# A gelu's inner product and a layer norm's factor and bias, from GpSimd to fused steps on VectorE

## The chip, the core and the metric

The kernel runs on one core of a Trainium2 chip. The metric is the time of one execution on the device in microseconds; a kernel's time is the median of several runs. The core's engines work side by side, each through its own list of instructions in order: TensorE (PE in the profile: matrix products, which need their weights loaded, PEld), VectorE (DVE), ScalarE (ACT), GpSimd (POOL) and SyncE (SP). They wait for each other through semaphores. TensorE writes to banks of PSUM; all else lies in SBUF. Transfers between memory and SBUF (DMA) are issued here from SyncE's and GpSimd's lists.

## What is computed

Two layers over 256 tokens of 2048 features. The first mixes a recurrence and a sparse attention; the second, which the change touches, is a gated unit. Its part of the reference:

```python
def odd_mixer(hn, w_in, ln_g, ln_b, w_s, b_s, w_out):
    u, v, g = jnp.split(hn @ w_in, 3, axis=-1)
    u = jax.nn.gelu(u)
    v = layer_norm(jax.nn.gelu(v), ln_g, ln_b)
    vc = v.reshape(bsz, n_chunks, SG_CHUNK, SG_GROUPS, SG_GROUP)
    mixed = jnp.einsum('gts,bcsgd->bctgd', ws, vc) + b_s.T[:, :, None]
    y = u * mixed.reshape(bsz, t, SG_WIDTH) * jax.nn.silu(g)
    return y @ w_out
```

The gelu is the tanh form, x (1 + tanh(c (x + a x^3))) / 2 with a = 0.044715. The layer norm takes the mean and the variance of each token over 2048 features, then a factor and a bias per feature. After each layer the input is joined by a gated embedding (`gate_layer`), with one more product by a 2048 x 2048 matrix.

## The kernel before, in words

**The weight stream.** Nearly all time goes to products of 256 tokens with wide weight matrices in float32, done in three fast passes: each operand is split in a high part (`hi`, `xh`) and a rest (`lo`, `xl`), and lines 169 to 171 add hi x xh, lo x xh and hi x xl. The weights come as a stream: SyncE loads 128 x 2048 numbers at a time (`raw`, line 128, five buffers), and each half of these is one chunk. For a chunk, ScalarE writes `hi` (line 137) and VectorE writes `lo = raw - hi` (line 138), each 128 x 1024 into one of four buffers; then TensorE has twelve matmuls on it (two token tiles, two weight tiles, three passes). Eight chunks make one unit, 512 features for all tokens, in two banks; its result goes to a background task.

**Background tasks.** Tasks are generators that `advance` moves one step for each chunk, so their instructions stand between those of the stream, on the same engines and in the same lists. The place in each engine's list is set by the order in which the program records them and by the scheduler of the tile framework.

**The second layer.** Four units give v (`ov_task`), four give u (`ou_task`), four the gate (`og_task`). Both `ov_task` and `ou_task` copy a unit's two tiles of 128 x 512 from the banks with the token's factor (`evac`, line 386) and call `gelu2` (line 696): ScalarE squares (702), VectorE scales and adds 1 (703), GpSimd multiplies by x (704), ScalarE takes the tanh (708), VectorE finishes (709). `ov_task` also gathers statistics on VectorE (720). When the fourth v unit is through, `ln` (726) turns these into a mean and a factor for each token, with a power on GpSimd (734); then for each of four column blocks `lng` and `lnb`, the factor and the bias for all partitions, are loaded from GpSimd's list (744), VectorE subtracts the mean and multiplies by the token's factor (748), and GpSimd multiplies by `lng` (749) and adds `lnb` (750). The first of these blocks fall into the time of the first u unit. `mix_task` needs both results; its first matmul (779) starts at 972.3 us of the profile.

Of the kernel before, what the change touches and what calls it, by code (L numbers as in the profile page):

```python
# [40 lines left out]
GELU_C = 0.7978845608028654  # L41
GELU_A = 0.044715

# columns of the packed parameter block
C_NG = 0
C_PG = 32
C_CW = 64
# [11 lines left out]
class Trunk:  # L59
# [13 lines left out]
        self.n = 0  # L73
        self.done = set()

# [1 line left out]
    def name(self, s):  # L77
        self.n += 1
        return f"{s}{self.n}"
# [13 lines left out]
    def pg(self, name="pg"):  # L93
        return self.psg.tile([128, 512], F32, tag="g", name=self.name(name))

# [1 line left out]
    def spawn(self, gen, delay=0):  # L97
        self.bg.append([delay, gen])

# [12 lines left out]
        while not all(k in self.done for k in keys):  # L112
            yield

# [1 line left out]
    def load(self, ap, cols):  # L116
        self.loads.append((ap, cols))
        return len(self.loads) - 1
# [29 lines left out]
            self.issue_split(self.next_split)  # L148
            self.next_split += 1

# [1 line left out]
    def unit(self, loads, acts, post, n=512, per_load=2, nk=KT, bank=None):  # L152
        st = {}
        bank = bank or self.pg
# [24 lines left out]
    def wunit(self, acts, post):  # L179
        self.unit([self.wl() for _ in range(4)], acts, post)  # L180

# [1 line left out]
    def split(self, src, gain=None, scale=None):  # L183
        """src [128 features, 2 tiles, 256 tokens] in two parts that the fast products carry exactly"""
        nc = self.nc
        hi = self.t(src.shape, F32R, "xh")
        lo = self.t(src.shape, F32R, "xl")
        if gain is not None:
            for s in range(2):
                g = gain[:, s:s + 1]  # L190
                nc.scalar.activation(hi[:, s], src[:, s], AF.Copy, scale=g)  # L191
                nc.vector.scalar_tensor_tensor(lo[:, s], src[:, s], g, hi[:, s].bitcast(F32),  # L192
                                               op0=OP.mult, op1=OP.subtract)
        elif scale is not None:
            nc.scalar.activation(hi, src, AF.Copy, scale=scale)
            nc.vector.scalar_tensor_tensor(lo, src, scale, hi.bitcast(F32), op0=OP.mult, op1=OP.subtract)
        else:
            nc.scalar.activation(hi, src, AF.Copy)
            nc.vector.tensor_tensor(lo, src, hi.bitcast(F32), op=OP.subtract)
        return hi, lo  # L200

    def fm(self, a0, a1, name="fm"):
        """token-major [128 tokens, 256] for both token tiles to [128 features, 2 tiles, 256 tokens] in a bank"""
        pt = self.pa(name)
        with self.tc.issue_after(self.last_mm.ins):
            for k in range(2):
                for t, x in ((0, a0), (1, a1)):
                    self.nc.tensor.transpose(pt[:, k * T + t * 128:k * T + (t + 1) * 128],  # L208
                                             x[:, k * 128:(k + 1) * 128], self.ident)
        return pt.rearrange("p (a b) -> p a b", a=2)  # L210

    def rms(self, ss, key):
        """ss [128 tokens, tile, part] of sums of squares"""
        nc = self.nc
        m = self.sm([128, 2])
        nc.vector.tensor_reduce(m, ss, axis=AX.X, op=OP.add)
        nc.vector.tensor_scalar(m, m, 1.0 / D, EPS, op0=OP.mult, op1=OP.add)  # L217
        r = self.kept([128, 4], "r" + key)
        nc.gpsimd.tensor_tensor(r[:, 0:2], m, self.mhalf[:, 0:2], op=OP.pow)  # L219
        nc.gpsimd.tensor_scalar(r[:, 2:4], r[:, 0:2], 0.5, None, op0=OP.mult)  # L220
        self.r[key] = r
        self.done.add("r" + key)
# [4 lines left out]
    def rth(self, key, t):  # L227
        return self.r[key][:, 2 + t:3 + t]

# [1 line left out]
    def consts(self):  # L231
        nc, a = self.nc, self.a
        self.cols = self.kept([128, C_ALL], "cols")
# [9 lines left out]
    def bias_table(self):  # L243
        nc, a = self.nc, self.a
        rel = self.kept([32, H], "rel")
        nc.gpsimd.dma_start(rel, a["rel_bias"])
        oh = self.kept([32, N_BUCKET_COLS], "oh")
        nc.gpsimd.dma_start(oh, a["onehot"])
        yield 4
        ps = self.pa("bt")  # L250
        with self.tc.issue_after(self.last_mm.ins):
            nc.tensor.matmul(ps[:H, :N_BUCKET_COLS], rel, oh, start=True, stop=True)
        sb = self.t([H, N_BUCKET_COLS], name="bt")
        nc.scalar.activation(sb, ps[:H, :N_BUCKET_COLS], AF.Copy)
        # row q of head h starts q elements further right: element (q, 127 + k) is the bias of key k
        bd = self.bias_d = self.dram.tile([H, 128, 512], F32, name="bias_d")
        yield
        nc.scalar.dma_start(bass.AP(tensor=bd.tensor, offset=bd.offset, ap=[[128 * 512, H], [513, 128], [1, 383]]),
                            sb[:, None, :383].to_broadcast([H, 128, 383]))
        self.done.add("bias")  # L260
# [26 lines left out]
        nc.vector.tensor_scalar(self.sp2, acc, 2.0, None, op0=OP.mult)  # L287
        nc.vector.tensor_scalar(self.spm4, acc, -4.0, None, op0=OP.mult)

# [1 line left out]
    def idx_task(self, i, ps):  # L291
        """the queries' own factor comes with iw, since relu(r x) = r relu(x) for r > 0"""
        nc = self.nc
        cp = lambda o, x: nc.scalar.activation(o, x, AF.Copy)
        if i == 0:
# [31 lines left out]
        yield  # L327

    def iq_task(self, j):
        """four heads"""  # L330
        nc = self.nc
        yield from self.until(f"iq{j // 2}")
        o = (j % 2) * T
# [44 lines left out]
        nc.vector.tensor_scalar(self.mb, sc, TAKEN_ABOVE, NEG, op0=OP.is_gt, op1=OP.mult)  # L378
        self.done.add("mask")

# [1 line left out]
    def evac(self, ps, key, name):  # L382
        out = []
        for t in range(2):
# [44 lines left out]
        self.done.add("v")  # L429
        yield  # L430

# [1 line left out]
    def q_task(self, g, ps):  # L433
        nc = self.nc
        qs = self.evac(ps, "x", "q")
# [87 lines left out]
        yield  # L523

    def gb_task(self, g, ps):
        """2 * silu without the token's factor, which comes with the attention"""
        nc = self.nc
        out = []
        for t in range(2):
            th = self.t(name="gb")  # L530
            nc.scalar.activation(th, ps[t], AF.Tanh, scale=self.rth("x", t))
            nc.vector.scalar_tensor_tensor(th, th, 1.0, ps[t], op0=OP.add, op1=OP.mult)
            out.append(th)
        self.sgb[g] = out
        self.done.add(f"gb{g}")
        yield

# [1 line left out]
    def ga_task(self, c, ps):  # L539
        nc = self.nc  # L540
        xs = self.evac(ps, "x", "ga")
# [82 lines left out]
        nc.vector.tensor_scalar(d, d, 0.0, -0.25, op0=OP.min, op1=OP.mult)  # L624
        st[p] = (a0, d, ti)

# [1 line left out]
    def squares(self, h, key, c, t):  # L628
        if c == 0 and t == 0:
            self.ss[key] = self.kept([128, 2, 4], "ss")  # L630
# [1 line left out]
        self.nc.scalar.activation(j, h, AF.Square, accum_out=self.ss[key][:, t, c:c + 1])  # L632

    def to_acts(self, hs, c, key, gain_col):
        """next products' operand; a step each"""
        for p in range(2):
            j = 2 * c + p
            o = p * T
# [53 lines left out]
        yield 2  # L692
        self.pT[layer] = {0: self.split(p)}

# [1 line left out]
    def gelu2(self, xs):  # L696
        """2 * gelu(x), in place, in steps"""
        nc = self.nc
        ys = []
        for x in xs:  # L700
            y = self.t(name="ge")
            nc.scalar.activation(y, x, AF.Square)  # L702
            nc.vector.tensor_scalar(y, y, GELU_A, 1.0, op0=OP.mult, op1=OP.add)  # L703
            nc.gpsimd.tensor_tensor(y, y, x, op=OP.mult)  # L704
            ys.append(y)
            yield
        for x, y in zip(xs, ys):
            nc.scalar.activation(y, y, AF.Tanh, scale=GELU_C)  # L708
            nc.vector.scalar_tensor_tensor(x, y, 1.0, x, op0=OP.add, op1=OP.mult)
            yield  # L710

# [14 lines left out]
    def ln(self):  # L726
# [12 lines left out]
        for c in range(4):  # L739
# [5 lines left out]
            yield  # L745
            for t in range(2):
                v = self.ov[c, t]
                nc.vector.tensor_scalar(v, v, mv[t][:, 0:1], sc[t][:, 1:2], op0=OP.subtract, op1=OP.mult)  # L748
                nc.gpsimd.tensor_tensor(v, v, g, op=OP.mult)
                nc.gpsimd.tensor_tensor(v, v, b, op=OP.add)  # L750
                yield
            self.done.add(f"vn{c}")

# [46 lines left out]
            self.y[2 * c + p] = self.split(self.fm(ys[0][:, o:o + T], ys[1][:, o:o + T], "yt"), scale=0.25)  # L800
        yield

# [1 line left out]
    def post(self, task, *args, delay=0):  # L804
        return lambda ps: self.spawn(task(*args, ps), delay)

# [188 lines left out]
```

## Time and profile before

| | |
|---|---|
| median of 3 runs | 1276.28 us (1275.89 to 1276.69) |
| span of the profiled execution, first to last instruction | 1273.7 us |
| TensorE busy | 1253.9 us (98%) |
| VectorE busy | 820.6 us (64%) |
| ScalarE busy | 679.9 us (53%) |
| GpSimd busy | 127.8 us (10%) |
| chain that ended last | PE 96%, DVE 2%, DMA 1%, issue 1% |
| DMA | 243.57 MB, mean 191 GB/s |

The profile is of one execution. Its busy times tell how full each engine is; its lists of waits tell what ended the idle time in front of an instruction; its timelines give start and length of single instructions. The length of a VectorE instruction includes time in which it has started and stands still. The time of the runs lies 2.6 us above the span, for what comes before the first and after the last instruction.

### The profile page before, as it was taken

What the parts mean: (1) busy time and instruction counts of PE and PEld (TensorE: products, weight loads), DVE (VectorE), ACT (ScalarE), POOL (GpSimd) and SP (SyncE); (2) the same over time, 40 slices, a digit from 0 to 9 for tenths busy, and PEclk for the clock granted to TensorE, in tenths of its full rate; (3) what the DMA queues carried; (4) which work ended last, traced back from release to release, by engine and by line L of the source; (5) the groups of instructions that cost most, each with busy time, mean ns of one, the idle gap of its engine ahead of it and who ended that gap; (6) DMA issues with size and microseconds to landing.
All of it is one profiled execution on the core that took longest, in us unless ns stands there. A gap on an engine that the chain in (4) does not pass through costs nothing.

```text
span 1273.7 us, 15432 instructions
## 1 busy us (share of the span) xinstructions
PE 1253.9 (98%) x5900; PEld 1045.2 (82%) x5900; DVE 820.6 (64%) x1176; ACT 679.9 (53%) x941; POOL 127.8 (10%) x130
## 2 busy tenths in 40 slices
PE   7999999999999999999999999999899999999998
PEld 7978888888888888888888888888688888888886
DVE  5658565667577777765556555666986666556554
ACT  6554454554577877843445555555445444545443
POOL 0000202113000100000000000112651000000000
PEclk9999999999999999999999999999999999999999
DMA  9975545445445455485555555565564544544650
GB/s 327 245 283 192 186 166 182 172 167 184 157 169 210 172 186 204 157 278 187 183 179 182 182 185 203 184 239 179 201 215 165 196 175 168 197 162 173 227 198 33
DMA packets 41963, 243.57 MB, mean 191 GB/s; under 512 B 4721, under 2 KB 7425, under 8 KB 16289
## 3 DMA queue, kind: packets, MB, share of 16 engines
q1 hardware_dynamic: 37296, 231.46, 51.5%
q0 software_dynamic: 2528, 7.99, 1.9%
q10 hardware_dynamic: 2064, 3.14, 1.5%
q8 instruction: 46, 0.75, 0.2%
q14 instruction: 29, 0.23, 0.0%
HBM read 237.33 MB, written 5.23 MB: 190 GB/s over the span
## 4 chain that ended last, share of the span: by engine, by line
PE 96%; DVE 2%; DMA 1%; issue 1%; ACT 0%; POOL 0%; SPq 0%; DVEq 0%; POOLq 0%
PE pg L169 29%; PE pg L170 29%; PE pg L171 29%; PE ht L208 1%; DVE lo L138 1%; PE pa L169 1%; PE pa L170 1%; PE pa L171 1%; PE mix L779 1%; PE lg L471 1%; PE sc L354 1%; DMA raw<-in_idx_w 0%; DMA x<-in_xT 0%; PE pt L500 0%; DVE v L748 0%
## 5 line engine op out<-in xcount | busy, mean ns | idle before, releaser
L138 DVE TENSOR_TENSOR lo<-raw,hi 128x1024 fp32r<-128x1024 f32 (+1 forms) x432 | 532.1, 1235 | 366.9 <-ACT hi L137 365.2
L137 ACT ACTIVATE hi<-raw 128x1024 fp32r<-128x1024 f32 (+1 forms) x432 | 450.5, 1045 | 503.5 <-PE pg L171 481.5
L169 PE MATMUL pg<-hi,xh 128*128 128x512 f32 (+1 forms) x1696 | 662.3, 391 | 7.0 <-ACT xh L191 6.6
L170 PE MATMUL pg<-lo,xh 128*128 128x512 f32 (+1 forms) x1696 | 657.5, 388 | 6.7 <-DVE lo L138 6.7
L171 PE MATMUL pg<-hi,xl 128*128 128x512 f32 (+1 forms) x1696 | 657.4, 388 | 0.0
L170 PEld LDWEIGHTS pg<-lo,xh 128*128 128x128 f32 x1696 | 319.7, 188 | 68.8 <-DVE lo L138 8.1
L169 PEld LDWEIGHTS pg<-hi,xh 128*128 128x128 f32 x1696 | 319.5, 188 | 68.8 <-ACT xh L191 6.6
L171 PEld LDWEIGHTS pg<-hi,xl 128*128 128x128 f32 x1696 | 319.3, 188 | 62.5
L219 POOL TENSOR_TENSOR rg<-s,mhalf 128x2 f32<-128x2 f32 x2 | 1.4, 720 | 296.6 <-DVE s L217 296.6
L568 POOL TENSOR_TENSOR tt<-tt,tg 128x512 f32<-128x512 f32 x8 | 10.4, 1296 | 202.5 <-ACT tt L566 202.5
L191 ACT ACTIVATE xh<-ht,cols 128x256 fp32r<-128x256 f32 x48 | 20.2, 473 | 8.5 <-PE ht L208 8.0
L192 DVE SCALAR_TENSOR_TENSOR xl<-ht,cols,xh 128x256 fp32r<-128x256 f32 x48 | 21.0, 479 | 3.7 <-ACT xh L191 3.3
L441 POOL TENSOR_TENSOR rq<-rq,mhalf 128x8 f32<-128x8 f32 x4 | 7.6, 1907 | 154.1 <-DVE rq L440 154.1
L592 DVE SCALAR_TENSOR_TENSOR xc<-xat,cols,xc 128x255 f32<-128x255 f32 (+2 forms) x48 | 22.2, 477 | 0.5
L703 DVE TENSOR_SCALAR ge<-ge 128x512 f32<-128x512 f32 x16 | 13.7, 856 | 10.7 <-ACT ge L702 10.1
L704 POOL TENSOR_TENSOR ge<-ge,v 128x512 f32<-128x512 f32 x8 | 14.3, 1788 | 61.6 <-DVE ge L703 61.6
L680 ACT ACTIVATE z<-pg,rg 128x512 f32<-128x512 f32 (+1 forms) x18 | 11.2, 641 | 14.8 <-PE pg L171 14.8
L704 POOL TENSOR_TENSOR ge<-ge,u 128x512 f32<-128x512 f32 x8 | 14.3, 1792 | 46.2 <-DVE ge L703 46.2
L708 ACT ACTIVATE ge<-ge 128x512 f32<-128x512 f32 x16 | 10.1, 633 | 14.9 <-POOL ge L704 14.9
L681 DVE SCALAR_TENSOR_TENSOR z<-z,pa 128x512 f32<-128x512 f32 (+1 forms) x18 | 11.0, 623 | 8.8 <-ACT z L680 8.8
L574 DVE TENSOR_TENSOR_SCAN hs<-a,tt 128x256 f32<-128x256 f32 x16 | 10.2, 677 | 9.1 <-POOL tt L568 9.1
L784 DVE SCALAR_TENSOR_TENSOR u<-mix,bs,u 128x128 f32<-128x128 f32 x32 | 9.0, 344 | 10.6 <-PE mix L779 10.6
(194 smaller groups left out, 825.4 us busy)
## 6 DMA issues: line engine op xcount, KB each, us to landing
raw<-in_w SPq DMA_DIRECT2D x200, 1024.0 KB, 4.8
raw<-in_idx_w SPq DMA_DIRECT2D x8, 736.0 KB, 7.4
raw<-in_pe_w SPq DMA_DIRECT2D x8, 512.0 KB, 3.7
bias_d<-bt ACTq DMA_DIRECT2D x1, 3064.0 KB, 38.2
raw<-in_idx_w SPq DMA_DIRECT2D x8, 368.0 KB, 6.1
x<-in_xT SPq DMA_DIRECT2D x8, 256.0 KB, 6.8
xn<-in_x SPq DMA_DIRECT2D x8, 256.0 KB, 7.8
bias<-bias_d POOLq DMA_DIRECT2D x8, 256.0 KB, 3.1
```

What stands on the lines that cost most here:

```text
L137: nc.scalar.activation(hi[:, :cols], raw, AF.Copy)
L138: lo_ins = nc.vector.tensor_tensor(lo[:, :cols], raw, hi[:, :cols].bitcast(F32), op=OP.subtract)
L169: self.nc.tensor.matmul(ps, xh, wh, start=(kt == 0), stop=False)
L170: self.nc.tensor.matmul(ps, xh, wl, start=False, stop=False)
L171: self.last_mm = self.nc.tensor.matmul(ps, xl, wh, start=False, stop=(kt == nk - 1))
L191: nc.scalar.activation(hi[:, s], src[:, s], AF.Copy, scale=g)
L192: nc.vector.scalar_tensor_tensor(lo[:, s], src[:, s], g, hi[:, s].bitcast(F32), op0=OP.mult, op1=OP.subtract)
L208: self.nc.tensor.transpose(pt[:, k * T + t * 128:k * T + (t + 1) * 128], x[:, k * 128:(k + 1) * 128], self.ident)
L354: nc.tensor.matmul(ps[b // 64][:, c0:c1], iq[b:b + 64, step, q0:q0 + 128], self.ik[b:b + 64, 0:c1 - c0], start=True, stop=True)
L592: nc.vector.scalar_tensor_tensor(xc[:, s, k:], xa[:, s, :T - k], col(C_CW + (3 - k) * 16 + f), xc[:, s, k:], op0=OP.mult, op1=OP.add)
L703: nc.vector.tensor_scalar(y, y, GELU_A, 1.0, op0=OP.mult, op1=OP.add)
L704: nc.gpsimd.tensor_tensor(y, y, x, op=OP.mult)
```

## The change

In `gelu2` the factor a is taken out of the inner sum: a x (1/a + x^2) instead of x (1 + a x^2). So (x^2 + 1/a) x is one step with two tensor operands on VectorE (a fused step, scalar_tensor_tensor), and a goes to the scale of ScalarE's tanh. In `ln` the order of the products changes: (v - mean) x `lng` is one fused step and (that) x token's factor + `lnb` the second, both on VectorE. GpSimd keeps the power and the loads.

```diff
     def gelu2(self, xs):
 ...
             nc.scalar.activation(y, x, AF.Square)
-            nc.vector.tensor_scalar(y, y, GELU_A, 1.0, op0=OP.mult, op1=OP.add)
-            nc.gpsimd.tensor_tensor(y, y, x, op=OP.mult)
+            nc.vector.scalar_tensor_tensor(y, y, 1.0 / GELU_A, x, op0=OP.add, op1=OP.mult)
 ...
-            nc.scalar.activation(y, y, AF.Tanh, scale=GELU_C)
+            nc.scalar.activation(y, y, AF.Tanh, scale=GELU_C * GELU_A)
 ...
                 v = self.ov[c, t]
-                nc.vector.tensor_scalar(v, v, mv[t][:, 0:1], sc[t][:, 1:2], op0=OP.subtract, op1=OP.mult)
-                nc.gpsimd.tensor_tensor(v, v, g, op=OP.mult)
-                nc.gpsimd.tensor_tensor(v, v, b, op=OP.add)
+                nc.vector.scalar_tensor_tensor(v, v, mv[t][:, 0:1], g, op0=OP.subtract, op1=OP.mult)
+                nc.vector.scalar_tensor_tensor(v, v, sc[t][:, 1:2], b, op0=OP.mult, op1=OP.add)
```

VectorE's list before, at the gelu of the first u unit (`ge`, `u`), behind the layer norm's steps of line 748; a name's number tells the tile:

```order
L138 TENSOR_TENSOR lo_7561<-raw_7510,hi_7560 128x1024
L703 TENSOR_SCALAR ge_7554<-ge_7554 128x512
L138 TENSOR_TENSOR lo_7587<-raw_7510,hi_7586 128x1024
L703 TENSOR_SCALAR ge_7582<-ge_7582 128x512
L709 SCALAR_TENSOR_TENSOR u_7550<-ge_7554,u_7550 128x512
L138 TENSOR_TENSOR lo_7610<-raw_7558,hi_7609 128x1024
L709 SCALAR_TENSOR_TENSOR u_7552<-ge_7582,u_7552 128x512
L138 TENSOR_TENSOR lo_7631<-raw_7558,hi_7630 128x1024
```

The same place in the changed kernel, whose `lo_7550` is the `lo_7561` above (lines 747 and 748 are the layer norm, 703 and 708 the gelu):

```order
L138 TENSOR_TENSOR lo_7550<-raw_7502,hi_7549 128x1024
L703 SCALAR_TENSOR_TENSOR ge_7544<-ge_7544,u_7540 128x512
L138 TENSOR_TENSOR lo_7575<-raw_7502,hi_7574 128x1024
L703 SCALAR_TENSOR_TENSOR ge_7571<-ge_7571,u_7542 128x512
L747 SCALAR_TENSOR_TENSOR v_7044<-v_7044,s_7470,lng_7567 128x512
L708 SCALAR_TENSOR_TENSOR u_7540<-ge_7544,u_7540 128x512
L748 SCALAR_TENSOR_TENSOR v_7044<-v_7044,s_7472,lnb_7568 128x512
L138 TENSOR_TENSOR lo_7597<-raw_7547,hi_7596 128x1024
L747 SCALAR_TENSOR_TENSOR v_7046<-v_7046,s_7476,lng_7567 128x512
L708 SCALAR_TENSOR_TENSOR u_7542<-ge_7571,u_7542 128x512
L748 SCALAR_TENSOR_TENSOR v_7046<-v_7046,s_7478,lnb_7568 128x512
L138 TENSOR_TENSOR lo_7617<-raw_7547,hi_7616 128x1024
```

The layer norm of the second column block now stands among the gelu's steps, between one `lo` and the next; the steps for the third and the fourth block follow in the same way between `lo_7639` and the `lo` behind `lo_7697`, four steps each.

GpSimd's list before, from the loads of the second block's factor and bias on:

```order
L744 DMA lng_7578<-in_ln_g 128x512
L744 DMA lnb_7579<-in_ln_b 128x512
L704 TENSOR_TENSOR ge_7554<-ge_7554,u_7550 128x512
L744 DMA lng_7646<-in_ln_g 128x512
L749 TENSOR_TENSOR v_7046<-v_7046,lng_7578 128x512
L704 TENSOR_TENSOR ge_7582<-ge_7582,u_7552 128x512
L750 TENSOR_TENSOR v_7046<-v_7046,lnb_7579 128x512
L749 TENSOR_TENSOR v_7048<-v_7048,lng_7578 128x512
L744 DMA lnb_7647<-in_ln_b 128x512
```

The same place in the changed kernel, from the two powers of `ln` (line 733 there) on:

```order
L733 TENSOR_TENSOR s_7472<-s_7472,mhalf_84 128x1
L733 TENSOR_TENSOR s_7478<-s_7478,mhalf_84 128x1
L743 DMA lng_7567<-in_ln_g 128x512
L743 DMA lnb_7568<-in_ln_b 128x512
L743 DMA lng_7632<-in_ln_g 128x512
L743 DMA lnb_7633<-in_ln_b 128x512
L743 DMA lng_7692<-in_ln_g 128x512
L743 DMA lnb_7693<-in_ln_b 128x512
```

The loads no longer stand behind products; the layer norm's steps that wait for them have moved to VectorE's list.

## Rows read from the trace of the kernel before

**Rows 1.** The page: the span, and each engine's busy time, share, instructions.

```profile
span 1273.7 us, 15432 instructions
...
PE 1253.9 (98%) x5900; PEld 1045.2 (82%) x5900; DVE 820.6 (64%) x1176; ACT 679.9 (53%) x941; POOL 127.8 (10%) x130
```

**Rows 2.** Waits of TensorE: who for whom, us in total, times, longest.

```profile
PE pg L170 <- DVE lo L138: 6.7, 4, 5.0
```

**Rows 3.** Windows of time: busy us of each engine in each stretch.

```profile
core 0: us, PE busy (x) PEld busy (x) DVE busy (x) ACT busy (x) POOL busy (x), PEclk, DMA share, GB/s
...
920.00:930.00 10.00, 5.75 (x17) 4.59 (x18) 10.00 (x4) 1.19 (x2) 9.96 (x9) 0.66 0.38 82
930.00:990.00 60.00, 60.00 (x275) 49.95 (x274) 44.08 (x43) 32.35 (x40) 16.44 (x9) 1.00 0.58 203
```

**Rows 4.** Timeline of TensorE, 908 to 927: start, length, instruction, [idle before <-releaser].

```profile
908.09 0.50 PE L170 MATMUL pg<-lo,xh 128*128 128x512 f32 x1 [0.95 <-DVE lo L138]
...
918.88 0.39 PE L169 MATMUL pg<-hi,xh 128*128 128x512 f32 x1
924.25 0.80 PE L170 MATMUL pg<-lo,xh 128*128 128x512 f32 x1 [4.98 <-DVE lo L138]
...
925.27 0.63 PE L169 MATMUL pg<-hi,xh 128*128 128x512 f32 x1
...
926.55 0.63 PE L169 MATMUL pg<-hi,xh 128*128 128x512 f32 x1
```

**Rows 5.** Timeline of ScalarE, 893 to 935: steps of line 137, x2 for two.

```profile
893.35 1.07 ACT L137 ACTIVATE hi<-raw 128x1024 fp32r<-128x1024 f32 x1 [0.92 <-PE pg L171]
...
904.23 1.06 ACT L137 ACTIVATE hi<-raw 128x1024 fp32r<-128x1024 f32 x1 [1.66 <-PE pg L171]
...
934.42 1.06 ACT L137 ACTIVATE hi<-raw 128x1024 fp32r<-128x1024 f32 x1 [1.66 <-PE pg L171]
```

**Rows 6.** Timeline of VectorE, 901 to 924.

```profile
901.64 2.32 DVE L138 TENSOR_TENSOR lo<-raw,hi 128x1024 fp32r<-128x1024 f32 x1
...
906.82 3.48 DVE L138 TENSOR_TENSOR lo<-raw,hi 128x1024 fp32r<-128x1024 f32 x3
...
913.96 5.46 DVE L709 SCALAR_TENSOR_TENSOR u<-ge,u 128x512 f32<-128x512 f32 x1 [1.84 <-ACT ge L708]
919.34 4.85 DVE L138 TENSOR_TENSOR lo<-raw,hi 128x1024 fp32r<-128x1024 f32 x1
```

**Rows 7.** Timeline of GpSimd, 895 to 927.

```profile
895.87 1.11 POOL L734 TENSOR_TENSOR s<-s,mhalf 128x1 f32<-128x1 f32 x2 [4.53 <-DVE s L733]
...
913.81 1.31 POOL L749 TENSOR_TENSOR v<-v,lng 128x512 f32<-128x512 f32 x1
...
918.80 0.58 POOL L744 DMA_DIRECT2D lnb<-in_ln_b  x1
919.40 1.28 POOL L750 TENSOR_TENSOR v<-v,lnb 128x512 f32<-128x512 f32 x1
...
923.05 0.58 POOL L744 DMA_DIRECT2D lng<-in_ln_g  x1
...
926.95 0.56 POOL L744 DMA_DIRECT2D lnb<-in_ln_b  x1
```

**Rows 8.** Single lines, in ns min/median/max; line 138 in the window 560 to 620.

```profile
L138 DVE TENSOR_TENSOR lo<-raw,hi x23: 1226/1226/1226, 560.0 to 619.8; 128x1024 fp32r<-128x1024 f32 x23
...
L709 DVE SCALAR_TENSOR_TENSOR u<-ge,u x8: 679/1764/5456, 914.0 to 989.7; 128x512 f32<-128x512 f32 x8
...
L703 DVE TENSOR_SCALAR ge<-ge x16: 414/429/1576, 821.1 to 984.2; 128x512 f32<-128x512 f32 x16
...
L796 DVE SCALAR_TENSOR_TENSOR og<-og,ro,u x8: 745/750/754, 1006.3 to 1081.3; 128x512 f32<-128x512 f32 x8
...
L704 POOL TENSOR_TENSOR ge<-ge,u x8: 1296/1751/2528, 910.7 to 985.9; 128x512 f32<-128x512 f32 x8
```

**Rows 9.** The tile `lng`: its four loads from issue to landing.

```profile
DMA to landing us min/median/max: 3.6/4.6/5.4
```

## The prediction, made before the changed kernel ran

> **What bounds the kernel now.** I read the page's busy line first: TensorE is busy for 1253.9 of 1273.7 us [rows 1]. The time of this kernel is the length of TensorE's row of matmuls plus the places where that row has a hole, so a change on VectorE or GpSimd can only matter through a hole. The second view is TensorE's own list of waits: 6.7 us in four waits for the low part of a weight chunk (`lo`, line 138), the longest 5.0 us [rows 2]; the other waits are start-up. The third view, the windows, places the hole: from 920 to 930 us TensorE is busy for 5.75 us and the granted clock is 0.66, while in the 60 us behind it is busy throughout at 1.00 [rows 3]. The timeline of TensorE shows the same place: one matmul starts at 918.88, the next at 924.25 after a wait of 4.98 us, and then groups of three matmuls come 1.28 us apart (925.27 to 926.55) [rows 4]. At the full rate three take 0.68 us, since a chunk of twelve passes in 2.72 us (below). So the hole has a tail at the lower of TensorE's two levels (1.2 instead of 2.4 GHz).
>
> **How long the hole is.** ScalarE makes the high part `hi` of a chunk (line 137) as soon as TensorE has left the buffer of four chunks earlier, so the starts of those steps are a clock of TensorE's progress. From 893.35 to 904.23 there are four steps in 10.88 us, 2.72 us a chunk. From 904.23 to 934.42 there are eight (the first and the last are shown; the six rows between hold seven more), where 8 x 2.72 = 21.76 us were due and 30.19 us went by [rows 5]. **The stretch loses 30.19 - 21.76 = 8.43 us**: about 5.9 us as the two waits that TensorE's timeline shows there (4.98 us, and one of 0.95 us at 908.09 [rows 4]), the other 2.5 us as restart and lower clock. All of it hangs on `lo` being late.
>
> **Why `lo` is late.** `lo` is one VectorE instruction. In a quiet stretch all 23 of them take 1226 ns [rows 8], and three in a row take 3.48 us together, some 1.16 us each [rows 6]. In the bad stretch one takes 4.85 us (from 919.34) and one 2.32 us; a fused step of line 709, whose fastest case is 679 ns [rows 8], takes 5.46 us (from 913.96) [rows 6]. Put GpSimd beside it: its products run back to back from 913.81, and the first thing that is not arithmetic on it is a DMA issue at 918.80; the VectorE step ends at 919.34, that is 0.5 us after. Products start again at 919.40, the next DMA issue is at 923.05, and `lo` ends at 919.34 + 4.85 = 924.19, 1.1 us after [rows 6, 7]. VectorE stood still until GpSimd's run of products had a gap, twice. Those two excesses are 4.8 and 3.6 us. TensorE goes on at 924.25, right behind that `lo`.
>
> Here a rule of the Trainium skill speaks against such long holds. SBUF — State Buffer, section Who interferes with whom, says that a VectorE instruction with two SBUF inputs shares a read port with a GpSimd instruction that reads SBUF, and that the later one blocks until the first finishes. The pairing is what the rows show; the length is not, since by the rule 5.46 us would have been about 2 us (one product and the step itself), and most of the hole would need another cause. What that cause would leave is the third rival.
>
> **The change part by part.**
> *Removed from GpSimd:* 16 products of the gelu and 16 of the layer norm, 1.3 to 2.5 us each as line 704 has them [rows 8]. Only ScalarE's tanh and, far later, the mixing products of line 779 need these results, so GpSimd's own time is worth nothing; what counts is that from the gelus to the end of the odd layer it has two tiny powers (1.11 us together [rows 7]) as its only arithmetic on tiles, so nothing can hold VectorE as above.
> *Added to VectorE:* 16 scalings of the gelu (median 429 ns [rows 8]) become 16 fused steps, and 8 of the layer norm become 16 fused steps. The trace does not show these very steps. The nearest rows are line 709 without GpSimd beside it, 679 ns, and line 796, which has two SBUF tensors and a factor per token as the new layer-norm steps have, 745 to 754 ns eight times over [rows 8]. I take 0.68 for the gelu and 0.75 for the layer norm; the lower end is 0.41 (the scaling now), the upper 1.76 (the median of line 709 where GpSimd works beside it [rows 8]).
> *Does it fit?* The order shows the densest place: from `lo_7550` up to the `lo` behind `lo_7697`, VectorE has eight `lo`, four gelu steps and twelve layer-norm steps. That is 8 x 1.16 + 4 x 0.68 + 12 x 0.75 = 9.3 + 2.7 + 9.0 = 21.0 us, and TensorE consumes eight chunks in 8 x 2.72 = 21.8 us. It fits by itself, and there is slack in front of it: `hi` starts three chunks (8.16 us) ahead of TensorE's need, `hi` takes 1.06 [rows 5] and `lo` 1.23 [rows 8], so VectorE may be late by **5.9 us** before TensorE sees it. Walking the new order with these lengths, the worst `lo` starts some 3 us after its `hi` is ready, behind three fused steps. So the added work costs nothing; its cover is this slack of 5.9 us. In the other gelus the margin is wider: two fused steps, no layer norm.
> *Moved:* the order of TensorE, ScalarE and SyncE is the same row for row but for buffer numbers and lines. On GpSimd's queue the six later loads of factor and bias no longer stand between products: all six follow the powers directly. The powers end near 895 to 897 [rows 7], six issues of 0.58 us follow, and with 3.6 to 5.4 us to landing [rows 9] they are in by 906. The first step that waits for one comes near 911 on VectorE, by the walk above, so the new wait costs nothing; its cover is some 5 us.
> *ScalarE's tanh* waits for VectorE instead of GpSimd and starts about 1 to 3 us sooner. It was hidden and stays hidden.
>
> **The sum.** 8.43 us are lost now, 0 after. In the profiled execution: span 1273.7 - 8.4 = 1265.3 us. The median of the runs, 1276.28, is 2.6 us above this span, and the runs differ by 0.8 us; what lies around the span does not change, so 1276.28 - 8.43 = **1267.9 us**.
>
> **Rivals.**
> *1. VectorE becomes the bound (slower).* If the 16 fused steps of the densest place take longer than thought, `lo` falls behind by itself. TensorE waits from 9.3 + 16 x = 21.8 + 5.9, that is from x = 1.15 us a step. For the end to be over 0.2% later than now, the new hole must exceed 8.4 + 2.6 = 11.0 us, some 2.5 of them clock: 9.3 + 16 x = 27.7 + 8.5, x = 1.68 us. At 1.76 us, as line 709 has it in the median, the stall is 37.5 - 27.7 = 9.8 us and with the clock 12.3: 1280.2 us. For it: that row exists. Against it: every such row has a GpSimd product beside it, and line 796 with the same operands takes 0.75 us.
> *2. The layer norm waits for its loads (partly given back).* VectorE now stands in order behind the landing of factor and bias, with the next `lo` queued behind, and TensorE behind that. If the loads were issued as late as now, the last bias (issued at 926.95 now) [rows 7] lands about 4.5 us later [rows 9] at 931.5 and the next `lo` ends at 931.5 + 0.75 + 1.23 = 933.5. Without the hole its `hi` would start seven chunks after 904.23, at 923.3, and TensorE would want it 8.2 later, at 931.5. That is 2.0 us: 1269.9. Against it: what held those issues were the products in front of them, which are gone.
> *3. The hole is not GpSimd's (no change).* If one product is all that GpSimd can hold, 5.46 us holds 5.46 - 0.68 - 1.3 = 3.5 us and 4.85 us holds 4.85 - 1.23 - 1.3 = 2.3 us of something that remains; 5.8 us of lag stay and with them the 4.98 us wait and its clock, about 7.2 us. Only 1.2 us come back: 1275.1. By the rule of the Trainium skill named above this is the case. Against it: both long steps end within 0.5 to 1.1 us of a gap in GpSimd's run and nothing else on VectorE is of such length outside it.
>
> **How the numbers follow.** Forecast 0.86; rival 2 0.04; rival 3 0.06; rival 1 0.04. A measurement of this kernel can tell about 0.2% (2.6 us) from no change. Forecast and rival 2 are faster: 0.90; rival 3 is within: 0.06; rival 1 is slower: 0.04. The range: the waits on `lo` add up to 6.7 us where 5.9 are in the stretch, so at best 0.8 more comes back, and with half the spread of the runs the low end is 1266.7; the high end takes in rival 2 and the spread, 1270.1.
>
> **What would show it.** In the profile after, right: TensorE's waits on `lo` between 820 and 1000 us are gone; a clock of 1.00 in every 10 us there; eight chunks of `hi` in some 21.8 us there, instead of 30.2; no `lo` above 1.3 us; fused steps of 0.68 to 0.75 us; span about 1265. Wrong: a `lo` with VectorE busy in front of it and TensorE waiting (rival 1), VectorE idle before a layer-norm step until a load lands (rival 2), or a VectorE step of several us with GpSimd idle (rival 3).

## The result, and the profile after

The changed kernel takes **1266.88 us** (median of 4 runs, 1266.74 to 1266.99), beside 1276.30 us for the kernel before (4 runs, 1275.89 to 1276.69). The ratio is 0.993, with a 95% interval of 0.9918 to 0.9941. The profiled span is 1265.2 us; 1265.3 was predicted. The page of the changed kernel (span; busy time, share and instructions of each engine), which answers to [rows 1]:

```profile
span 1265.2 us, 15394 instructions
...
PE 1251.8 (99%) x5900; PEld 1044.7 (83%) x5900; DVE 798.7 (63%) x1184; ACT 679.1 (54%) x941; POOL 73.6 (6%) x98
```

GpSimd lost 54 us of work. VectorE has eight instructions more and is still busy for 22 us less: what it had been charged for was partly time in which it stood still. TensorE's waits in the changed kernel (who for whom, us in total, times, longest), beside [rows 2]:

```profile
PE pg L169 <- ACT xh L191: 6.2, 1, 6.2
...
PE pg L170 <- DVE lo L138: 0.5, 1, 0.5
```

The 6.7 us on `lo` have shrunk to one wait of 0.5 us, which like the 6.2 us above it lies at the start of the program. Windows of the changed kernel, beside [rows 3] (busy us and instructions of each engine, granted clock, DMA share, GB/s):

```profile
core 0: us, PE busy (x) PEld busy (x) DVE busy (x) ACT busy (x) POOL busy (x), PEclk, DMA share, GB/s
...
910.00:920.00 10.00, 10.00 (x46) 8.29 (x45) 10.00 (x14) 4.80 (x6) 0.00 (x0) 1.00 0.48 171
920.00:930.00 10.00, 10.00 (x46) 8.29 (x45) 8.21 (x11) 5.20 (x7) 0.00 (x0) 1.00 0.70 251
```

From 910 to 920 us VectorE has no free moment, and TensorE does not notice: it is busy throughout, at a clock of 1.00. ScalarE's steps of line 137, which tell TensorE's progress, stand at (beside [rows 5])

```profile
904.20 1.06 ACT L137 ACTIVATE hi<-raw 128x1024 fp32r<-128x1024 f32 x1 [1.66 <-PE pg L171]
...
912.36 1.07 ACT L137 ACTIVATE hi<-raw 128x1024 fp32r<-128x1024 f32 x1 [0.76 <-PE pg L171]
...
925.96 1.06 ACT L137 ACTIVATE hi<-raw 128x1024 fp32r<-128x1024 f32 x1 [1.65 <-PE pg L171]
```

The last of these is the eighth step after 904.20: 21.76 us, where 30.19 us went by before. VectorE's timeline in the same stretch of the changed kernel, beside [rows 6]:

```profile
909.11 1.23 DVE L138 TENSOR_TENSOR lo<-raw,hi 128x1024 fp32r<-128x1024 f32 x1 [0.26 <-ACT hi L137]
910.26 0.69 DVE L703 SCALAR_TENSOR_TENSOR ge<-ge,u 128x512 f32<-128x512 f32 x1
...
915.84 2.36 DVE L138 TENSOR_TENSOR lo<-raw,hi 128x1024 fp32r<-128x1024 f32 x2
918.11 1.42 DVE L747 SCALAR_TENSOR_TENSOR v<-v,s,lng 128x512 f32<-128x512 f32 x2
...
926.16 0.76 DVE L748 SCALAR_TENSOR_TENSOR v<-v,s,lnb 128x512 f32<-128x512 f32 x1
```

From 909.11 to 926.92 us it works without a gap: seven `lo`, three gelu steps and twelve layer-norm steps. None of them is long. The worst `lo` here is the first of the two at 915.84: its `hi` was ready at 912.36 + 1.07 = 913.43, so it starts 2.4 us late, within the 5.9 us that were there.

### The profile page after: what moved, and what is told of

It is laid out like the page before. It is cut to its first block, busy times and chain, and to the rows that moved or that the text cites. A ratio compares the mean times of both kernels' runs of the same rounds, so it can differ in the third digit from the quotient of the medians.

```text
span 1265.2 us, 15394 instructions
## 1 busy us (share of the span) xinstructions
PE 1251.8 (99%) x5900; PEld 1044.7 (83%) x5900; DVE 798.7 (63%) x1184; ACT 679.1 (54%) x941; POOL 73.6 (6%) x98
## 4 chain that ended last, share of the span: by engine, by line
PE 98%; DMA 1%; DVE 0%; ACT 0%; SPq 0%; POOL 0%; issue 0%; DVEq 0%; POOLq 0%
PE pg L169 30%; PE pg L171 30%; PE pg L170 30%; PE ht L208 1%; PE pa L170 1%; PE pa L171 1%; PE pa L169 1%; PE mix L777 1%; PE lg L471 1%; PE sc L354 1%; DMA raw<-in_idx_w 0%; DMA x<-in_xT 0%; PE pt L500 0%; PE yt L208 0%; PE gate L605 0%; PE gate L606 0%
## 5 line engine op out<-in xcount | busy, mean ns | idle before, releaser
L138 DVE TENSOR_TENSOR lo<-raw,hi 128x1024 fp32r<-128x1024 f32 (+1 forms) x432 | 522.9, 1213 | 381.2 <-ACT hi L137 380.0
L490 ACT ACTIVATE L<-L,s 128x256 f32<-128x256 f32 (+1 forms) x32 | 14.2, 445 | 3.1 <-DVE s L484 3.1
L632 ACT ACTIVATE junk<-xr 128x512 f32<-128x512 f32 x24 | 15.2, 635 | 0.0
L208 PEld LDWEIGHTS ht<-ident,xr 128*128 128x128 f32 x96 | 11.0, 140 | 5.1 <-DVE xr L664 2.1
L208 PE MATMUL ht<-ident,xr 128*128 128x128 f32 x96 | 14.9, 278 | 0.0
```

The source lines that it names most:

```text
L138: lo_ins = nc.vector.tensor_tensor(lo[:, :cols], raw, hi[:, :cols].bitcast(F32), op=OP.subtract)
L490: nc.scalar.activation(L[h][:, c0:c1], L[h][:, c0:c1], AF.Exp, bias=mx[:, x:x + 1], accum_out=sm[:, x:x + 1])
```

## The experiments

What was open behind the number is the cause: why VectorE stood still twice, and which part of the change removed that. The theory was the prediction's: a run of GpSimd's products holds VectorE until it has a gap. The rival: one product at most holds it, and something else makes the long steps. The kernel before was run again beside each group of runs: 1276.19 us (median of 7) beside the first eight, 1275.3 (one run) beside the next three, 1275.46 (median of 11) beside the last. Where only one run is given, the differences read are well above the 2.5 us over which single runs of the kernel before spread (1274.78 to 1277.31), or they are read from the trace.

**Each half alone.** Only the layer norm's part of the change:

```diff
-                nc.vector.tensor_scalar(v, v, mv[t][:, 0:1], sc[t][:, 1:2], ...)
-                nc.gpsimd.tensor_tensor(v, v, g, op=OP.mult)
-                nc.gpsimd.tensor_tensor(v, v, b, op=OP.add)
+                nc.vector.scalar_tensor_tensor(v, v, mv[t][:, 0:1], g, ...)
+                nc.vector.scalar_tensor_tensor(v, v, sc[t][:, 1:2], b, ...)
```

> The kernel before, with only the layer norm's factor and bias as two fused steps on VectorE; the gelu's inner product stays on GpSimd. Theory (a run of GpSimd products without a gap holds VectorE, and the layer norm makes the long run): GpSimd has at most two products in a row left, VectorE is late by under 5.9 us, the hole is gone: 1266.9 us, as with the whole change, and span 1265.2. Rival (the gelu's chain of VectorE, GpSimd, ScalarE and back to VectorE makes the lag): the chain stands as before, so most of the 8.4 us stay: about 1275 us.

Measured: 1267.14 us (4 runs, 1266.81 to 1267.67), ratio 0.993 (0.9914 to 0.9947), as expected. Only the gelu's part:

```diff
-            nc.vector.tensor_scalar(y, y, GELU_A, 1.0, op0=OP.mult, op1=OP.add)
-            nc.gpsimd.tensor_tensor(y, y, x, op=OP.mult)
+            nc.vector.scalar_tensor_tensor(y, y, 1.0 / GELU_A, x, op0=OP.add, op1=OP.mult)
```

> The kernel before, with only the gelu's inner product as a fused step on VectorE; the layer norm's factor and bias stay on GpSimd. Theory: the layer norm's products now follow each other on GpSimd with even fewer gaps (up to eight in a row), VectorE stands still for several us at a time, and a hole of 5 us or more with a lower clock stays: 1272 to 1279 us. Rival (the gelu's chain makes the lag): the chain is short now, no hole: 1267 us.

Measured: 1267.27 us (4 runs, 1266.79 to 1267.89), ratio 0.993 (0.9915 to 0.9945). Either half brings the whole gain, so the halves don't add up: each takes away something that the hole needs. The second run was a miss of the theory, since sixteen products of the layer norm were still on GpSimd. Its trace (GpSimd, then VectorE) shows why:

```profile
908.87 3.93 POOL L748 TENSOR_TENSOR v<-v,lng 128x512 f32<-128x512 f32 x2 [3.19 <-DMA lng<-in_ln_g]
912.77 3.44 POOL L749 TENSOR_TENSOR v<-v,lnb 128x512 f32<-128x512 f32 x2
```

```profile
909.34 2.32 DVE L138 TENSOR_TENSOR lo<-raw,hi 128x1024 fp32r<-128x1024 f32 x1
911.58 1.77 DVE L703 SCALAR_TENSOR_TENSOR ge<-ge,u 128x512 f32<-128x512 f32 x1
913.27 1.78 DVE L708 SCALAR_TENSOR_TENSOR u<-ge,u 128x512 f32<-128x512 f32 x1
```

Here GpSimd's products follow each other, and VectorE does not stand still until they end. The two **take turns, one instruction each**: a VectorE step costs some 1.1 us more (1.78 for 0.69, 2.32 for 1.23), and a product takes 1.7 to 2.0 us in the mean of two instead of 1.3. This is the rule of the Trainium skill, SBUF — State Buffer, section Who interferes with whom, that the later of the two blocks until the first finishes; these rows agree with it. So the rival's premise was right here, and the prediction's "stood still until GpSimd's run had a gap" was not a rule.

**A run of products by itself.** The changed kernel with eight more products on GpSimd, between two tiles of the layer norm's result (the results are not used), and the same with two fills of 128x256 behind every second product:

```diff
+        p, q = self.ov[3, 0], self.ov[3, 1]
+        z = [self.t(name="zz") for _ in range(8)]
+        for i in range(8):
+            nc.gpsimd.tensor_tensor(z[i], p, q, op=OP.mult)
```

> The changed kernel, with eight extra products of 128 x 512 on GpSimd, in a row, whose results nobody reads; they start when the layer norm's last step is done, near 927 us, and last some 10 us. Nobody waits for them. Theory: VectorE stands still in one or two steps of 4 us and more until the run is over, lag up to 10 us against a slack of 5.9: a hole of 3 to 5 us and a lower clock behind it, span 1268 to 1272 us. Rival (one GpSimd product holds one VectorE step at most, 1.3 us): seven or eight VectorE steps in the stretch are some 1 us longer each, lag below 5.9 us, no hole: span 1265.2 us.

> As the kernel with eight extra GpSimd products in a row behind the layer norm, but two fills of 128 x 256 (no operand read) stand behind every two products. Theory: VectorE gets in at each pair of fills, no step of it is longer than two products and itself (about 3.8 us), no hole or one below 1 us: span 1265 to 1266 us. If a fill holds VectorE like a product, the run is longer than without the fills, and so is the hole: span above that of the kernel without fills.

Measured: 1267.69 and 1267.74 us. GpSimd's row in the first of these two:

```profile
926.64 14.90 POOL L754 TENSOR_TENSOR zz<-v,v 128x512 f32<-128x512 f32 x8 [26.64 <-ACT hi L137]
```

Turns again (1.86 us a product, VectorE's steps 1.77 and 2.31 us). Of a hole there is one wait of 0.6 us, at 942.67, and gaps make no difference. A run of products alone does not hold VectorE.

**Gaps in the run of the kernel before.** The kernel before, with a fill of 128x256 behind each product of the layer norm:

```diff
+                    with self.tc.issue_after(i.ins):
+                        nc.gpsimd.memset(self.gap, 0.0)
```

> The kernel before, with a fill of 128 x 256 on GpSimd (no operand read) behind nearly every layer-norm product; VectorE's list is the same. GpSimd has more to do. Either half of the change alone had removed the hole, and with extra products in a row VectorE and GpSimd took turns one by one; so a run without a gap does not by itself hold VectorE. Theory (in the kernel before VectorE misses its turn between back-to-back products, and any step of GpSimd that reads nothing lets it in): no VectorE step above 2.5 us in 910 to 925, hole below 1 us, span near 1266 us. Rival (the hole comes from the order of the gelu's and the layer norm's products, which stands): span 1272 to 1276 us.

Measured: 1275.54 us; the hole stays (TensorE busy for 7.11 us from 920 to 930, clock 0.83). GpSimd, then VectorE:

```profile
915.24 0.58 POOL L745 DMA_DIRECT2D lng<-in_ln_g  x1
915.84 1.31 POOL L751 TENSOR_TENSOR v<-v,lng 128x512 f32<-128x512 f32 x1
...
918.32 0.32 POOL L753 MEMSET gap<- 128x256 f32 x1
...
919.82 0.32 POOL L753 MEMSET gap<- 128x256 f32 x1
...
921.33 0.31 POOL L753 MEMSET gap<- 128x256 f32 x1
921.60 1.47 POOL L751 TENSOR_TENSOR v<-v,lnb 128x512 f32<-128x512 f32 x1
```

```profile
915.99 5.95 DVE L709 SCALAR_TENSOR_TENSOR u<-ge,u 128x512 f32<-128x512 f32 x1 [1.84 <-ACT ge L708]
```

VectorE's step stands still through two fills, against the theory that any gap lets it in. It ends at 921.94, 0.6 us behind the start of the third fill, so that one did let it in; and a `lo` that began at 927.98 and took 2.45 us got in at the first fill behind it (929.26). A fill can end a standstill, then, but does not always. The run of products itself begins right behind a **load issue** (915.24), as both runs in [rows 7] that held VectorE do: 919.40, behind 918.80, and 913.81, behind an issue that [rows 7] leave out:

```profile
913.21 0.58 POOL L744 DMA_DIRECT2D lng<-in_ln_g  x1
```

That became the new theory. It fits the two halves: with either alone, no product follows directly behind an issue (the wait of 3.19 us for a load lies between in the rows above, 0.45 us in the layer norm's half).

**The issue taken away.** The kernel before, with the eight loads of factor and bias issued from SyncE's list:

```diff
-                nc.gpsimd.dma_start(x, bass.AP(...))
+                nc.sync.dma_start(x, bass.AP(...))
```

> The kernel before, with the loads of factor and bias issued from SyncE's list instead of GpSimd's. VectorE's list is the same; GpSimd has the same products, one pair in another order, and no DMA issue between them. Theory 1 (the two standstills begin right behind a DMA issue on GpSimd and end at the next one, so a DMA issue puts the two engines out of step): VectorE and GpSimd take turns, no step above 2.5 us, span 1265 to 1267 us. Theory 2 (VectorE misses its turn whenever the gelu's and the layer norm's products mix on GpSimd, and a DMA issue is what lets it in): fewer gaps, longer standstill, span 1274 us or more.

Measured: 1271.87 us. The same two places on VectorE, 913.96 and 919.34 before:

```profile
913.95 0.69 DVE L709 SCALAR_TENSOR_TENSOR u<-ge,u 128x512 f32<-128x512 f32 x1 [1.84 <-ACT ge L708]
914.90 1.23 DVE L138 TENSOR_TENSOR lo<-raw,hi 128x1024 fp32r<-128x1024 f32 x1 [0.26 <-ACT hi L137]
920.47 1.10 DVE L709 SCALAR_TENSOR_TENSOR u<-ge,u 128x512 f32<-128x512 f32 x1 [4.35 <-ACT ge L708]
921.49 13.47 DVE L138 TENSOR_TENSOR lo<-raw,hi 128x1024 fp32r<-128x1024 f32 x6
```

The standstill is gone. Some 5 us of the gain are missing for another reason: the loads are issued later (909.57 to 913.37) among those of `raw`, the second gelu product waits on GpSimd behind layer-norm products, VectorE idles 4.35 us, and six `lo` then take turns at 2.25 us each. TensorE still waits on `lo` three times between 900 and 950 us: 0.75 us (at 908.08), 1.86 us (at 923.85) and 0.81 us (at 944.20).

**The issue put back.** The changed kernel with one extra product, a load issue, four products, a load issue and three products (their results are not used):

```diff
+        last = nc.gpsimd.tensor_tensor(z[0], p, q, op=OP.mult)
+        for i in range(1, 10):
+            with self.tc.issue_after(last.ins):
+                if i in (1, 6):
+                    last = nc.gpsimd.dma_start(z[i], bass.AP(...))
+                else:
+                    last = nc.gpsimd.tensor_tensor(z[i], p, q, op=OP.mult)
```

> The changed kernel with extra work on GpSimd behind the layer norm, near 927 us, whose results nobody reads: one product, a load issue of 256 KB, four products, a load issue, three products. With eight products and no load issue the engines took turns and the span was 1265.9 us. Theory 1 (a DMA issue puts the engines out of step): behind the first issue VectorE stands still for four products, a step of 4 us or more, and a hole of 1 to 3 us: span 1267 to 1269. Theory 2 (the issue has no such effect): they take turns, span 1265.5 to 1266 us.

Measured: 1274.63 us: **the hole is back, in a kernel that had lost it.** VectorE, GpSimd, and the windows:

```profile
929.65 9.92 DVE L703 SCALAR_TENSOR_TENSOR ge<-ge,u 128x512 f32<-128x512 f32 x1 [1.64 <-ACT ge L702]
```

```profile
929.10 0.58 POOL L758 DMA_DIRECT2D zz<-in_ln_g  x1
929.70 5.03 POOL L760 TENSOR_TENSOR zz<-v,v 128x512 f32<-128x512 f32 x4
934.68 0.58 POOL L758 DMA_DIRECT2D zz<-in_ln_g  x1
935.28 3.73 POOL L760 TENSOR_TENSOR zz<-v,v 128x512 f32<-128x512 f32 x3
```

```profile
930.00:940.00 10.00, 6.76 (x30) 5.26 (x28) 10.00 (x2) 1.49 (x3) 8.99 (x8) 1.00 0.21 56
940.00:950.00 10.00, 8.63 (x25) 6.87 (x26) 7.14 (x8) 4.88 (x7) 0.00 (x0) 0.66 0.67 220
```

The products run at full speed (1.26 us each) and one VectorE step stands still for 9 us, past the second issue too. It cost more than expected for that reason.

**The issue, or the moment?** The first product also began just when VectorE's step did. Three runs separate this: (a) one issue and then eight products without another; (b) each issue replaced by a fill of 128x512, of nearly the same length; (c) a fill of 128x256 in front of the first issue, so that VectorE's step begins during the issue and ahead of the product. The edits to the loop above:

```diff
 a:             if i in (1, 6):          ->  if i == 1:
 b:   last = nc.gpsimd.dma_start(z[i], ...)  ->  last = nc.gpsimd.memset(z[i], 0.0)
 c: + if i == 1:
    +     last = nc.gpsimd.memset(z[10][:, 0:256], 0.0)
```

> The changed kernel with one extra product of two old tiles on GpSimd, one load issue behind it, and then eight extra products (128x512) without a further issue; the extra results are not used. Theory A, a run of products that starts right behind a load issue holds VectorE until the run ends: one VectorE step of some 10.5 us (8 x 1.25 and the step itself) beside eight products at 1.25 us each, span 1271 to 1276. Theory B, the hold has a limit of about four products (5 us), which is the longest seen so far: one VectorE step of some 5.4 us, then turns one by one (1.77 and 2.3 us a VectorE step), span 1266 to 1269.

> The run behind load issues, with each of the two load issues replaced by a fill of 128x512 on GpSimd of about the same length (0.55 to 0.6 us), so that the products start at the same moment relative to VectorE's step. Theory A, the load issue brings the hold: turns one by one here, VectorE steps of 1.77 and 2.3 us, span 1266. Theory B, the hold comes when a VectorE step and the first product begin within some 0.2 us of each other, whatever stood before: one or two VectorE steps of 5 us beside products at 1.25 us each, span 1271 to 1275.

> The run behind load issues, with a fill of 128x256 (0.3 us) in front of the first load issue, so that the issue stands directly before the products as there, but VectorE's step begins during the issue, some 0.3 us ahead of the first product instead of 0.05 us. Theory A, the load issue brings the hold whatever the moment: one or two VectorE steps of 5 us, span 1271 to 1275. Theory B, the moment of the start decides: the first VectorE step 0.7 us, then turns (1.77 and 2.3 us), span 1266.

Measured: (a) 1275.59, (b) 1268.32, (c) 1273.99 us. VectorE's first step at this place, in the order a, b, c:

```profile
930.10 10.56 DVE L703 SCALAR_TENSOR_TENSOR ge<-ge,u 128x512 f32<-128x512 f32 x1 [1.64 <-ACT ge L702]
```

```profile
929.85 1.78 DVE L703 SCALAR_TENSOR_TENSOR ge<-ge,u 128x512 f32<-128x512 f32 x1 [1.64 <-ACT ge L702]
```

```profile
929.78 10.16 DVE L703 SCALAR_TENSOR_TENSOR ge<-ge,u 128x512 f32<-128x512 f32 x1 [1.64 <-ACT ge L702]
```

In (b) VectorE's step begins 0.06 us behind the first product (929.79) and waits for that one product alone. In (c) it begins 0.31 us ahead of the first product (930.09), during the issue (929.49 to 930.07), and stands still for 9.5 us. The moment of (b) lies between those of the standstills, 0.31 us ahead of the first product in (c) and 0.15 us behind it in the kernel before (913.96 and 913.81). So the issue decides, not the moment, and in (a) the hold lasts through all eight products. It is not the transfer that holds: the load of (a) landed 3.3 us after its issue at 929.55, and the step stood still until about 940. Eight products without an issue gave a span of 1265.9; (a), with one product and one issue ahead of the eight, gives 1273.8, and (b), with fills, 1266.5: the issue, an instruction of 0.58 us, costs over 7 us.

**Is VectorE near its limit?** The changed kernel with eighteen more fused steps on VectorE, three for each token tile of the last three blocks of the layer norm (their result is not used):

```diff
+                if c > 0:
+                    for _ in range(3):
+                        nc.vector.scalar_tensor_tensor(self.junk, g, 1.0, b, op0=OP.add, op1=OP.mult)
```

> The changed kernel with 18 extra fused steps of 128 x 512 on VectorE in the layer norm's last three blocks, results unused. This doubles the disputed load: 18 x 0.68 = 12 us in the place where I counted some 0.3 us free and 5.9 us of slack, so VectorE falls behind by about 12 us. If the slack is 5.9 us: TensorE waits about 6 us and the clock falls behind it, span 1271 to 1274 us. If the slack were under 3 us: more than 9 us and clock, span 1276 or more. If VectorE had free time that I did not see: span below 1268.

Measured: 1268.36 us, span 1266.6: 1.4 us lost, less than expected. VectorE has no gap from 909.65 to 948.0 us, and `lo` starts up to 8.3 us late. TensorE hides most of it because the scheduler placed mixing products there, which the changed kernel does at 963.8 us at the earliest. TensorE in this run:

```profile
929.80 0.83 PE L781 MATMUL mix<-v,ws 128*128 128x128 f32 x6
...
935.96 1.27 PE L781 MATMUL mix<-v,ws 128*128 128x128 f32 x10
...
939.84 1.95 PE L781 MATMUL mix<-v,ws 128*128 128x128 f32 x16
```

These are 4.05 us of TensorE's work brought forward. So the run shows that VectorE is not the bound in the changed kernel and has room for several us more; it does not measure the threshold, since the order of TensorE's list moved with it.

**The issues moved ahead, the products left.** The kernel before, with all eight loads issued from GpSimd's list ahead of the layer norm's first product:

```diff
+        gb = []
+        for c in range(4):
+            gb.append([self.t(name="lng"), self.t(name="lnb")])
+            for x, src in zip(gb[c], ("ln_g", "ln_b")):
+                nc.gpsimd.dma_start(x, bass.AP(...))
 ...
-            g = self.t(name="lng")
-            b = self.t(name="lnb")
 ...
+            g, b = gb[c]
```

> The kernel before, with all products left on GpSimd and only the eight load issues of factor and bias moved, on GpSimd's own list, ahead of the layer norm's first product, so that no issue stands between products any more. Theory A, the hole comes from products right behind a load issue: no VectorE step of several us, VectorE and GpSimd take turns one by one (lo 2.3 us beside products), TensorE's waits on lo below 1 us, span 1265 to 1267, time 1267 to 1269: nearly all of the gain without moving any work to VectorE. Theory B, the products beside the weight stream cost by themselves: a hole of several us stays somewhere in 880 to 940 us, time 1270 to 1276.

Measured: 1279.28 us (8 runs, 1278.28 to 1279.99), ratio 1.0029 (1.0018 to 1.0040): **slower** than the kernel before by 0.3%. No step stands still, as theory A said of the mechanism, but its time is wrong, and theory B's range is passed too. VectorE's rows:

```profile
898.66 4.33 DVE L750 TENSOR_SCALAR v<-v,s,s 128x512 f32<-128x512 f32 x3
902.90 2.31 DVE L138 TENSOR_TENSOR lo<-raw,hi 128x1024 fp32r<-128x1024 f32 x1
905.14 5.76 DVE L750 TENSOR_SCALAR v<-v,s,s 128x512 f32<-128x512 f32 x4
910.83 6.71 DVE L138 TENSOR_TENSOR lo<-raw,hi 128x1024 fp32r<-128x1024 f32 x3
917.46 2.95 DVE L703 TENSOR_SCALAR ge<-ge 128x512 f32<-128x512 f32 x2
920.33 2.31 DVE L138 TENSOR_TENSOR lo<-raw,hi 128x1024 fp32r<-128x1024 f32 x1
```

With the loads there early, sixteen products follow each other from 897.6 to 925 us beside VectorE's burst. In these 24 us VectorE gets fourteen steps done, each some 1.0 us longer than alone (5 x 1.16 + 9 x 0.43 = 9.7 us alone, by [rows 6] and, for lines 750 and 703, the 429 ns of [rows 8]); only five of them are `lo`, where TensorE consumes a chunk in 2.72 us. TensorE is busy for 21.6 of the 30 us from 900 to 930. Its longest wait there, and a row of ScalarE:

```profile
913.16 0.52 PE L170 MATMUL pg<-lo,xh 128*128 128x512 f32 x1 [4.85 <-DVE lo L138]
```

```profile
926.29 0.63 ACT L708 ACTIVATE ge<-ge 128x512 f32<-128x512 f32 x1 [15.51 <-POOL ge L704]
```

The wait of 4.85 us is for a `lo` that is late by turns. So turns alone can make a hole too, when there are enough of them in one place. A second part has another cause: the gelu's product stands on GpSimd behind all sixteen, ScalarE waits 15.51 us for it in front of the tanh, the next `hi` stands behind that tanh, and TensorE then waits 2.2 us for `hi` (at 927.92).

## Why the prediction was right, point by point

*Place, size and cover of the hole: right.* 8.43 us were to come back in the span; 1273.7 - 1265.2 = 8.5 did, at the place that was named, with the clock at 1.00. One part of the 5.9 us of waits does not belong to the standstills: the 0.95 us at 908.09 come before both, and with the loads on SyncE's list, where nothing stands still, 0.75 us of them stay.

*The price of the added steps: right.* 0.75 us was taken for the layer norm's steps and 0.68 for the gelu's. Single lines of the changed kernel (ns min/median/max), beside [rows 8]:

```profile
L747 DVE SCALAR_TENSOR_TENSOR v<-v,s,lng x8: 681/752/755, 894.2 to 923.7; 128x512 f32<-128x512 f32 x8
L748 DVE SCALAR_TENSOR_TENSOR v<-v,s,lnb x8: 749/753/755, 897.3 to 926.2; 128x512 f32<-128x512 f32 x8
L703 DVE SCALAR_TENSOR_TENSOR ge<-ge,u x8: 687/690/694, 908.2 to 975.9; 128x512 f32<-128x512 f32 x8
L138 DVE TENSOR_TENSOR lo<-raw,hi x65: 1209/1226/1228, 822.6 to 999.3; 128x1024 fp32r<-128x1024 f32 x65
```

The seven `lo` and fifteen fused steps from 909.11 on took 17.8 us, where the same walk gives 7 x 1.16 + 3 x 0.68 + 12 x 0.75 = 19.2: steps that follow each other begin some 0.09 us before the one in front is recorded as ended, and the walk counted that only for `lo`. Rival 1 is out by these rows and by the run with eighteen more steps.

*The loads: no price, as said, but the landing was mis-sized.* They were to land within 5.4 us and be in by 906. Issued one behind the other from 897.19 to 899.88, they took 3.8, 5.3, 5.4, 6.8, 9.4 and 12.2 us, in this order. Landing of `lng`, then of `lnb`, beside [rows 9] (with the first block's, issued at 814.6 and 815.1):

```profile
DMA to landing us min/median/max: 3.8/4.6/9.4
```

```profile
DMA to landing us min/median/max: 5.3/6.4/12.2
```

So the last two were in at 908.7 and 912.1 only. Nothing waited: the first pair, in at 901.0 and 903.1, is first read at 910.86 and 912.12, and the last pair at 923.04 and 924.36. The cover of the first step was 9 us or more, where some 5 us were predicted. Rival 2 stays out.

*The cause: half right.* That GpSimd's products held VectorE stands: without them, or with the issues elsewhere, both long steps are gone, and one issue in front of products brings them back. The step that failed is "VectorE stood still until GpSimd's run of products had a gap". Usually the two take turns; the standstill comes where products follow directly behind a load issue on GpSimd's list, and neither a fill nor a second issue ends it every time. The rule of the Trainium skill named above does not cover this: a VectorE step of 10.56 us beside eight products goes against it, and the measurement decides. Rival 3's premise, one product at most, holds elsewhere; its price was wrong because the two long steps of the kernel before lie behind issues. The number survived since the change takes away every product near an issue, whatever the rule; that a wrong rule led to it is luck. With the prediction's rule alone, one would have foretold a hole of several us for the eight plain products (there is one wait of 0.6 us), and an end of it with fills (it stays).

*The time around the span: mis-sized.* The 2.6 us were taken from the median of the runs and the span of one profiled execution, which was a faster one. Where a run's own time and span are both on record, they lie 1.7 to 1.9 us apart, in 18 runs of the kernel before as in the four of the changed kernel. So this time did not change, but a span of 1273.7 goes with some 1275.5 us, and the median run of the kernel before has about 0.8 us more in its span than the profile shows. That is most of the 1.0 us between the predicted 1267.9 and the measured median, which lies only 0.2 us above the low end of the range. In which stretch the median run loses these 0.8 us, no trace shows.

*What stays open.* Why a load issue has this effect, and what ends a standstill before the run of products ends: in the kernel before, the two ended at the next issue; behind the extra issue of the run that put it back, it lasted past one; with fills, one ended at the third and one at the first. In each of the seven cases seen, VectorE's step began during the issue or up to 0.18 us behind it; at two other issues of the kernel before (923.05 and 926.95 in [rows 7]) a `lo` had already begun, and turns followed. That is a pattern in the rows, not a tested cause. No run beat the changed kernel; neither half alone can be told from it.

## What to carry to other kernels

A VectorE step that reads two tensors from SBUF, beside products on GpSimd, costs a product more per step (some 1.1 us here); count these steps in the densest place and compare with the slack of the engine that waits. Look on GpSimd's list for products directly behind a load issue: there one VectorE step can stand still for the whole run of them (10.56 us for eight). Before moving work between engines, see whether half of the change does it, and before moving only the loads, see what will then start sooner and where.

## What the runs showed of the hardware

- Turns: beside GpSimd products of 128x512, VectorE steps of 0.69 and 1.23 us take 1.78 and 2.31 us, and a product goes from 1.26 us to about 1.9 us.
- Behind a load issue on GpSimd, the products keep 1.24 to 1.31 us each, and a VectorE step that began during the issue or up to 0.18 us behind it took 2.45 us (one product, then a fill) to 10.56 us (eight products); with a fill of 128x512 (0.52 us) in the issue's place it took 1.78 us.
- Of the fills of 128x256 (0.32 us) between the products, in the kernel before, two in a row did not let VectorE in; the third did.
- Six loads of 128x512 issued within 3.2 us took 3.8 to 12.2 us to land, each longer than the one before, beside at most 5.4 us for `lng` and 5.0 us for `lnb` when they were spread.
